# End of the second MLP: four plain blocks moved between the fifth and sixth block product, weights left unscaled, gate and residual one tile behind

## The chip, the core and the metric

The kernel runs on one core of a Trainium2 chip. The metric is device microseconds of one execution. A core has five engines, each with its own instruction queue, worked off in order: TensorE (PE in the profile, its weight loads PEld) multiplies matrices into PSUM, eight banks of 128 x 512 numbers; VectorE (DVE), ScalarE (ACT) and GpSimd (POOL) compute on tiles in SBUF, and only DVE and ACT read PSUM here; SyncE (SP) issues the loads. Stores of the output are issued on ACT's queue.

## What the kernel computes

A two-layer network over 1024 latent rows and 256 context rows of width 1024. Each layer has a token mixer and an MLP, each with a gated residual and a layer norm behind it. What this case is about is the very end, the MLP of the second layer, where only the latent rows are left:

```
h  = square(relu(modulate(x, sh2, sc2) @ w_up))      # 1024 x 4096
m  = h @ w_down                                      # 1024 x 1024
y  = alpha * x + g2 * m                              # g2: one row of 1024 gates, alpha = 2**0.5
out = (y - mean(y)) * rsqrt(var(y) + 1e-5) * ln2_g + ln2_b
```

## The kernel before

**Exact products from three.** Each float32 matrix is split into a rounded part "hi" and a rest "lo"; a product is three matmuls, hi x hi, hi x lo and lo x hi (`mm3`, lines 233 to 236). The split costs a copy on ACT and a subtraction (`lo`, line 230) on DVE or POOL.

**Block products.** `down_blocks` (it starts at line 2045) computes most of `h @ w_down` with seven products in place of eight per pair of blocks. The inner dimension is cut into seven groups (28 of the 32 slices of 128), and four slices are left for plain products at the end. In a group the seven products come in the order 1, 5, 6, 3, 2, 7, 4, each for four row tiles: 7 x 7 x 4 = 196 steps of six matmuls (128 x 512). `form` prepares the operands of a product two products ahead, with one or two POOL instructions, two ACT copies and a DVE subtraction. A step's result is added to the output half tile `acc` by DVE (`evac`, line 2237), two steps behind. Products 1, 6, 7 and 4 use the four banks x, products 5, 3 and 2 the four banks y; the banks keep running sums, so a step waits until the step before on its bank has been added to `acc`. Product 2 is the last that adds to row tiles 0 to 3; products 7 and 4 add to tiles 4 to 7.

**The order of the work.** Everything is under a manual schedule: each engine carries out its instructions in the order in which the program names them. Work of the end is hung onto the last steps by the dictionary `tail`, from step number (N is 196) to calls: loading and scaling the four last slices of `w_down`, splitting them and the four last slices of `h`, and the gate and residual of the first tiles.

**The end before.** `wm` (line 2179) multiplies a slice of `w_down` by the gate row on POOL (line 2182), then splits it. So the plain product comes out gated, and the gate must also be put on what the seven groups have summed: `fold` (line 2168) does it for one row tile, with a POOL multiplication (line 2171) and a DVE residual addition `alpha * x + y` (line 2172). `fold` of tiles 0 to 3 stands in `tail` at steps N-8, N-6, N-3 and N-2; that of tile t+4 at the head of tile t in `finish_last`. `finish_last` then does, for the eight row tiles in turn, 24 matmuls in two halves, DVE adds each half to `acc` (line 2335) and takes statistics (`bn_stats`, line 2336), `stats` (lines 1264 to 1270) makes mean and rstd with three small DVE and two small POOL instructions, ACT normalizes (line 2316), POOL multiplies by `ln2_g` (line 2318), DVE adds `ln2_b` (line 2321), and the tile is stored. The last tile ends on DVE alone (lines 2346 and 2348). The eight banks are used in turn.

**Buffers.** `s5` tiles (a in the profile) come from 25 buffers, `s4` tiles (b) from 20; a load waits until a buffer is free.

Of the kernel before, what the change touches and what calls it, by code (L numbers as in the profile page):

```python
# [10 lines left out]
F32 = mybir.dt.float32  # L11
F32R = mybir.dt.float32r
AF = mybir.ActivationFunctionType
ALU = mybir.AluOpType
# [4 lines left out]
D = 1024  # L19
SEQ = 1024  # L20
# [7 lines left out]
ALPHA = (2 * DEPTH) ** 0.25  # L28
# [49 lines left out]
def host_layout(a):  # L78
# [3 lines left out]
    o["xn"] = xa  # L82
    o["xT"] = xa.T.reshape(KT, 128, TOK)
    o["cT"] = np.stack([a["c"][0], a["c_ctx"]], 0).reshape(2, KT, 128).transpose(2, 1, 0)
# [18 lines left out]
    o["lnc"] = ln.reshape(2, 4, KT, 128).transpose(3, 0, 1, 2)  # L103
    o["sub"] = a["subln_w"].T
    o["dl"] = a["diff_lambda"].reshape(1, 512)
# [41 lines left out]
class Prog:  # L147
# [81 lines left out]
    def lo(self, out, x, hi, eng=None):  # L229
        (eng or self.nc.vector).tensor_tensor(out, x, hi, op=ALU.subtract)  # L230
# [181 lines left out]
    def first_xmod(self):  # L412
# [50 lines left out]
        def part(kt, u, k=0):  # L463
            for s, o in PS[u][k:]:
                self.mm3(o, W[u][0][:, kt], W[u][1][:, kt], X[kt][0][:, s], X[kt][1][:, s], kt == 0, kt == KT - 1)

# [10 lines left out]
        self.in_push(0)  # L477
        W = []
        for i in range(KT + 2):
# [3 lines left out]
            if i == 1:  # L483
                W = [self.wget(), self.wget()]
            loads(i + 2)
            if i == 2:
                W.append(self.wget())
            if i == 5:
# [34 lines left out]
    def pre(self, X, groups, per, ahead=0):  # L523
        ws = [self.wget() for _ in range(2)]
        self.wq_fill(ahead)
        ps = [None, None]
        for g in groups:
            if g is None:
                yield True
                continue  # L530
            for i, c, w in g:
                if ps[i] is None:
                    ps[i] = self.p3()
                for kt in range(KT):
                    xh, xl = X[kt]
                    self.mm3(ps[i][:, c:c + w], ws[i][0][:, kt], ws[i][1][:, kt], xh[:, c:c + w], xl[:, c:c + w],
                             kt == 0, kt == KT - 1)
                    if kt % per == per - 1:
                        yield False
        self.ready = ps  # L540
# [160 lines left out]
    def fourier2(self, b, n):  # L701
        nc = self.nc
        P = n // 256
        dm = self.dm
# [36 lines left out]
        for k in range(1, P):  # L741
# [3 lines left out]
            yield  # L745
        s2(P - 1)
        yield
# [370 lines left out]
    def attention_steps(self, l):  # L1118
# [34 lines left out]
        for i in range(N + LAG + 1):  # L1153
            T = []
            k = i - LAG
            if 0 <= k < N:
# [3 lines left out]
                E, Ec = st[k][0], st[k][2]  # L1160
                T = [self.att_T(E, Ec and Ec[0], st["aT", kh, kqb], kb, g) for g in range(3)]

            def t(g):
                if g < len(T):
                    next(T[g])

# [147 lines left out]
    def out_proj_setup(self, l):  # L1314
        nc = self.nc
        n = TOK if l == 0 else SEQ
        T = n // 128
        W, ld, gs, X2, xr, ys, s6, P = {}, {}, {}, [], {}, {}, {}, {}
        st = {}
# [24 lines left out]
        def mms(t, c, kts):  # L1344
# [7 lines left out]
            for kt in kts:  # L1352
                if kt not in W:
                    W[kt] = self.wget()
# [692 lines left out]
    def down_blocks(self, l, NG):  # L2047
        nc = self.nc
        n = SEQ if l else TOK
        T, HB, NB = n // 128, n // 2, D // 2  # L2050
        act, v, g = nc.scalar, nc.vector, nc.gpsimd
# [9 lines left out]
        acc = [None] * T  # L2061
# [82 lines left out]
        f = form(*seq[0])  # L2144
# [12 lines left out]
        bk = {"x": [self.p1() for _ in al], "y": [self.p1() for _ in range(8 - TH)]}  # L2157
        W, H, S, HR = [], [], [], []
        xr = {}
        self.acc = acc  # L2160
        gate = lambda t: self.gs[int(t >= 8)][:, :D]

        def rload(t):
            if t < T:
                xr[t] = self.s5()
                self.load(xr[t][:, :D], self.X2d[t])

        def fold(t):
            if t < T:
                y = acc[t]  # L2170
                g.tensor_tensor(y, y, gate(t), op=ALU.mult)
                v.scalar_tensor_tensor(y, xr.pop(t)[:, :D], ALPHA, y, op0=ALU.mult, op1=ALU.add)
                rload(t + 2)

        def wl(f):
            raw = self.s5()
            self.load(raw[:, :D], self.a["wd"][l, f])
            S.append(raw[:, :D])

        def wm():  # L2180
            raw = S.pop(0)
            g.tensor_tensor(raw, raw, gate(0), op=ALU.mult)
            hi, lo = self.s4(F32R), self.s4(F32R)
            act.copy(hi, raw)
            self.lo(lo, raw, hi)
            W.append((hi, lo))

        def whi():
            hi, lo = self.s4(F32R), self.s4(F32R)
# [7 lines left out]
        def hraw(f):  # L2197
            raw = self.s5()
            self.load(raw[:, :n], self.HL[f])
            HR.append(raw[:, :n])  # L2200

        def hconv():
            raw = HR.pop(0)
            hi, lo = self.s5(F32R), self.s5(F32R)
            act.copy(hi[:, :n], raw)
            self.lo(lo[:, :n], raw, hi[:, :n], g)
            H.append((hi, lo))

        def hl(f):
            hraw(f)  # L2210
            hconv()

        def gload(v=0):
            self.gs[v] = self.bcast(self.grow[(l, 5, v)], self.s5()[:, :D])

        n = SEQ if l else TOK
        N = len(prods)
        P = lambda fn, *a: (lambda: fn(*a))
        if l:
            tail = [[gload], [P(wl, 0)], [P(wl, 1), wm], [P(wl, 2), wm], [P(wl, 3), wm],  # L2220
                    [wm, P(rload, 0), P(rload, 1)], [P(hl, 0), P(hl, 1)], [P(fold, 0), P(hl, 2), P(fold, 1)],
                    [P(hl, 3), P(fold, 2), P(fold, 3)]]
            tail = {N - 4 * (9 - a) + b: f for a, fs in enumerate(tail) for b, f in enumerate(fs)}
        else:
            tail = {-20: P(wl, 0), -18: P(wl, 1), -16: whi, -15: wlo, -14: P(wl, 2), -13: whi, -12: wlo,
                    -11: P(hraw, 0), -10: whi, -9: wlo, -8: hconv, -7: P(hraw, 1), -6: P(wl, 3), -5: hconv,
                    -4: [P(hraw, 2), P(hraw, 3)], -3: [gload, P(rload, 0)], -2: hconv, -1: whi}
            tail = {N + k: f for k, f in tail.items()}
# [12 lines left out]
        for k, (n_, i, t) in enumerate(prods):  # L2241
# [8 lines left out]
            b, w = where(i, t)  # L2250
            ps = bk[b][w]
            evac(lag, ps)
            prod(n_, i, t, ps, i in (1, 5, 2))
            r, c = to[i]
# [9 lines left out]
                self.later()  # L2264
        evac(0)
        if l:
            self.lastW = W
            self.finish_last(l, H, lambda: None, bk["x"] + bk["y"], lambda t: fold(t + 4))
            yield
            return  # L2270
        wlo()
# [21 lines left out]
                self.wlo()  # L2293
            self.wrdy.append((hi, lo))

    def finish_last(self, l, H, lo, banks, pre):
        nc = self.nc
        T = SEQ // 128
        lg = self.bcast(self.a["lnr"][l, 2:3])
        lb = self.bcast(self.a["lnr"][l, 3:4])  # L2300
        W = self.lastW
        P = {}
        halves = (slice(0, 512), slice(512, 1024))

        def mm(t, c, r):
            sl = slice(128 * t, 128 * t + 128)
            if (t, c) not in P:
                P[t, c] = banks[(2 * t + c // 512) % 8]
            for i in r:
                self.mm3(P[t, c], H[i][0][:, sl], H[i][1][:, sl], W[i][0][:, c:c + 512], W[i][1][:, c:c + 512],  # L2310
                         i == 0, i == 3)

        def fin1(t):
            r, m, _ = st.pop(t)
            y = self.acc[t]
            nc.scalar.activation(y, y, AF.Identity, bias=m, scale=r)
            o[t] = self.s4()
            nc.gpsimd.tensor_tensor(o[t], y, lg, op=ALU.mult)

        def fin2(t):  # L2320
            nc.vector.tensor_tensor(o[t], o[t], lb, op=ALU.add)
            self.store(self.out[128 * t:128 * t + 128], o.pop(t))

        st, o = {}, {}
        for t in range(T):
            pre(t)
            y = self.acc[t]
            s6 = self.sm([128, 2, 6], bufs=3)
            if t == 0:
                mm(0, 0, range(3))  # L2330
                mm(0, 512, range(3))
                lo()
            for k, c in enumerate((0, 512)):
                mm(t, c, range(3, 4) if t == 0 else range(4))
                nc.vector.tensor_tensor(y[:, c:c + 512], P.pop((t, c)), y[:, c:c + 512], op=ALU.add)
                nc.vector.bn_stats(s6[:, k], y[:, c:c + 512])
                if k == 0 and t:
                    fin1(t - 1)
                if k == 0 and t > 1:
                    fin2(t - 2)  # L2340
            if t == T - 1:
                fin2(t - 1)
            st[t] = r, _, mean = self.stats(s6)
        x = self.s4()
        for c in halves:
            nc.vector.scalar_tensor_tensor(y[:, c], y[:, c], mean, lg[:, c], op0=ALU.subtract, op1=ALU.mult)
        for c in halves:
            nc.vector.scalar_tensor_tensor(x[:, c], y[:, c], r, lb[:, c], op0=ALU.mult, op1=ALU.add)
            self.store(self.out[128 * t:128 * t + 128, c], x[:, c])

    def finish(self, l):
        with self.tc.manual_schedule():
# [165 lines left out]
```

## Times and profile before

| what | us |
| --- | --- |
| median of three runs (lowest, highest) | 2947.97 (2942.29, 2949.51) |
| the profiled execution | 2943.8 |
| its span, first to last instruction | 2941.9 |
| PE busy in the span | 2743.8 (93%) |
| DVE busy | 2015.1 (68%) |
| ACT busy | 1149.9 (39%) |
| POOL busy | 1099.0 (37%) |

Times in the rows are microseconds from the start of the span. In a row of the timeline the columns are start, duration, engine, line, operation, output and inputs by kind of tile (q is a PSUM bank, a and b the SBUF tiles, c small ones), shape and count; in brackets the idle time before it and what ended it. A matmul row of 0.39 at the full clock overlaps the next, which starts 0.23 later. The last group's product 2 starts at 2849.28 and the plain blocks at 2875.54, where the output's input changes from a,a to b,a.

### The profile page before, as it was taken

What the parts mean: (1) busy time and instruction counts of PE and PEld (TensorE: products, weight loads), DVE (VectorE), ACT (ScalarE), POOL (GpSimd) and SP (SyncE); (2) the same over time, 40 slices, a digit from 0 to 9 for tenths busy, and PEclk for the clock granted to TensorE, in tenths of its full rate; (3) what the DMA queues carried; (4) which work ended last, traced back from release to release, by engine and by line L of the source; (5) the groups of instructions that cost most, each with busy time, mean ns of one, the idle gap of its engine ahead of it and who ended that gap; (6) DMA issues with size and microseconds to landing.
All of it is one profiled execution on the core that took longest, in us unless ns stands there. A gap on an engine that the chain in (4) does not pass through costs nothing.

```text
span 2941.9 us, 37767 instructions
## 1 busy us (share of the span) xinstructions
PE 2743.8 (93%) x14290; PEld 2347.7 (80%) x14290; DVE 2015.1 (68%) x2915; ACT 1149.9 (39%) x1608; POOL 1099.0 (37%) x664
## 2 busy tenths in 40 slices
PE   7889989889989999899999999999899999999986
PEld 5788878778779999788887788888777788878865
DVE  6667768845467787677776455667744677668887
ACT  4221156623343444533332321256523455553331
POOL 2511135633100000166665610146755000068795
PEclk9999999999999999999999999999899999999998
DMA  7244653337546555644344245662355565554451
GB/s 261 83 152 143 182 131 82 100 126 247 203 162 219 170 178 170 222 141 144 130 154 143 76 149 161 194 149 74 108 177 172 194 223 194 202 201 156 145 191 58
DMA packets 228745, 468.16 MB, mean 159 GB/s; under 512 B 18926, under 2 KB 116692, under 8 KB 228564
## 3 DMA queue, kind: packets, MB, share of 16 engines
q1 hardware_dynamic: 208392, 394.39, 41.5%
q10 hardware_dynamic: 17292, 61.93, 5.5%
q0 software_dynamic: 2880, 9.44, 0.8%
q8 instruction: 113, 1.85, 0.3%
q14 instruction: 68, 0.56, 0.1%
HBM read 322.36 MB, written 143.31 MB: 158 GB/s over the span
## 4 chain that ended last, share of the span: by engine, by line
PE 68%; DVE 11%; issue 6%; POOL 5%; DMA 5%; ACT 4%; SPq 1%; ACTq 0%; DVEq 0%; POOLq 0%
PE q L234 14%; PE q L236 14%; PE q L235 14%; PE p L234 5%; PE p L236 5%; PE p L235 5%; PE q L1025 3%; PE p L955 2%; PE p L956 2%; PE q L1012 2%; DVE c L958 2%; DVE a L230 1%; POOL a L230 1%; DVE b L230 1%; DMA d<-a 1%
## 5 line engine op out<-in xcount | busy, mean ns | idle before, releaser
L234 PE MATMUL q<-a,a 128*128 128x512 f32 (+1 forms) x1610 | 587.9, 365 | 34.9 <-DVE b L2237 13.7
L236 PE MATMUL q<-a,a 128*128 128x512 f32 (+2 forms) x1658 | 601.2, 363 | 5.0 <-DVE a L230 5.0
L235 PE MATMUL q<-a,a 128*128 128x512 f32 (+1 forms) x1594 | 581.6, 365 | 3.2 <-POOL a L230 3.2
L235 PE MATMUL p<-a,b 128*128 128x512 f32 (+1 forms) x1088 | 408.4, 375 | 1.1 <-POOL a L230 1.0
L234 PEld LDWEIGHTS q<-a,a 128*128 128x128 f32 x1610 | 305.2, 190 | 82.7 <-DVE t L1952 10.8
L236 PEld LDWEIGHTS q<-a,a 128*128 128x128 f32 x1658 | 314.2, 190 | 49.6 <-DVE a L230 7.4
L230 POOL TENSOR_TENSOR a<-b,a 128x256 fp32r<-128x256 f32 (+1 forms) x137 | 220.1, 1614 | 345.1 <-ACT a L2098 193.6
L2237 DVE TENSOR_TENSOR b<-q,b 128x512 f32<-128x512 f32 x405 | 268.7, 684 | 110.8 <-PE q L236 109.7
L235 PEld LDWEIGHTS q<-a,a 128*128 128x128 f32 x1594 | 302.4, 190 | 45.3 <-POOL a L230 4.3
L234 PE MATMUL p<-a,b 128*128 128x512 f32 (+1 forms) x816 | 307.7, 377 | 13.6 <-ACT b L2290 8.5
L236 PE MATMUL p<-a,b 128*128 128x512 f32 (+1 forms) x800 | 295.3, 369 | 4.0 <-DVE b L230 4.0
L230 DVE TENSOR_TENSOR a<-a,a 128x1024 fp32r<-128x1024 f32 (+4 forms) x163 | 266.7, 1639 | 38.3 <-ACT a L2095 27.5
L234 PE MATMUL q<-b,a 128*128 128x256 f32 (+1 forms) x748 | 256.7, 343 | 18.6 <-ACT b L604 8.4
L235 PE MATMUL q<-b,a 128*128 128x256 f32 (+1 forms) x748 | 253.8, 339 | 0.9 <-DVE b L230 0.9
L339 DVE SCALAR_TENSOR_TENSOR m<-w,k,m 128x256 f32<-128x256 f32 x448 | 227.4, 519 | 39.2 <-DMA w<-wmr 29.9
L236 PE MATMUL q<-b,a 128*128 128x256 f32 (+1 forms) x748 | 253.6, 339 | 0.0
L235 PEld LDWEIGHTS p<-a,b 128*128 128x128 f32 x1088 | 209.3, 192 | 34.2 <-POOL a L230 1.9
L958 DVE TENSOR_REDUCE c<-p 128x1 f32<-128x1280 f32 x128 | 190.5, 1488 | 63.1 <-PE p L956 61.9
L989 ACT ACTIVATE a<-p,c 128x1280 f32<-128x1280 f32 x128 | 170.4, 1331 | 89.8 <-DVE c L958 80.7
L234 PEld LDWEIGHTS p<-a,b 128*128 128x128 f32 x816 | 157.5, 193 | 39.3 <-ACT b L2290 9.3
L236 PEld LDWEIGHTS p<-a,b 128*128 128x128 f32 x800 | 153.9, 192 | 32.2 <-DVE b L230 7.0
L234 PEld LDWEIGHTS q<-b,a 128*128 128x128 f32 x748 | 144.8, 194 | 41.0 <-ACT b L604 11.4
(302 smaller groups left out, 5410.7 us busy)
## 6 DMA issues: line engine op xcount, KB each, us to landing
a<-d SPq DMA_DIRECT2D x86, 512.0 KB
w<-wmr SPq DMA_DIRECT2D x160, 256.0 KB
a<-d SPq DMA_DIRECT2D x56, 640.0 KB
b<-wu SPq DMA_DIRECT2D x64, 512.0 KB
d<-t SPq DMA_DIRECT2D x46, 640.0 KB
b<-wd SPq DMA_DIRECT2D x52, 512.0 KB
d<-a ACTq DMA_DIRECT2D x40, 640.0 KB
a<-d SPq DMA_DIRECT2D x80, 320.0 KB
```

The source lines that it names most:

```text
L230: (eng or self.nc.vector).tensor_tensor(out, x, hi, op=ALU.subtract)
L234: mm(out, lh, rh, start=start, stop=False, skip_group_check=on)
L235: mm(out, lh, rl, start=False, stop=False, skip_group_check=on)
L236: mm(out, ll, rh, start=False, stop=stop, skip_group_check=on)
L339: nc.vector.scalar_tensor_tensor(a, w[:, i], s, a, op0=ALU.mult, op1=ALU.add)
L955: nc.tensor.matmul(ps[:, c:c + w], Q[p][:, qs], K[p][0][:, ks], start=True, stop=False)
L956: nc.tensor.matmul(ps[:, c:c + w], Q[p][:, qs], K[p][1][:, ks], start=False, stop=True)
L958: nc.vector.reduce_max(mx, ps[:, :nkey], axis=AX.X, negate=True)
L989: self.nc.scalar.activation(e[:, :nkey], ps[:, :nkey], AF.Exp, bias=mx, accum_out=s)
L1012: nc.tensor.transpose(pt[:, i], e, self.ident)
L1025: nc.tensor.matmul(po[:, :256], V[i // 8][:, i % 8], aT[i // 4][:, i % 4], start=i == 0, stop=i == 9)
L2237: v.tensor_tensor(a, ps, a, op=ALU.add)
```

## The change

`wm` and `fold` go. The four slices of `w_down` are split unscaled (`whi`, `wlo`), and loads and splits of weights and `h` stand earlier in `tail`, from step N-26 to N-10. `finish_last` no longer does work when called: it returns `step`, and its calls are spread. After step N-9, the last of product 2, come the waiting additions and then the plain blocks of tiles 0 to 3 on the four banks y (steps 0 to 3 of `last`). Product 7 and 4 follow, with `last(4)` behind step N-8 and `last(5)` behind step N-6. After the loop come tiles 4 to 7 and the end, on all eight banks.

In a step for tile t, PE does the 24 matmuls and DVE adds the two halves; between the halves DVE does the residual of tile t-1; then come the statistics of tile t-1, the gate of tile t on POOL (now on the whole sum), the normalization and POOL's multiplication by `ln2_g` for tile t-1, and DVE's addition of `ln2_b` and the store for tile t-2. The last tile's gate and residual are on DVE, by halves. `ln2_g` and `ln2_b` lie in `s5` tiles, which are named before the loop over the steps.

```diff
-        gate = lambda t: self.gs[int(t >= 8)][:, :D]
...
-        def fold(t):
...
-        def wm():
...
         if l:
-            tail = [[gload], [P(wl, 0)], [P(wl, 1), wm], [P(wl, 2), wm], [P(wl, 3), wm],
-                    [wm, P(rload, 0), P(rload, 1)], [P(hl, 0), P(hl, 1)], [P(fold, 0), P(hl, 2), P(fold, 1)],
-                    [P(hl, 3), P(fold, 2), P(fold, 3)]]
-            tail = {N - 4 * (9 - a) + b: f for a, fs in enumerate(tail) for b, f in enumerate(fs)}
+            tail = {-26: P(wl, 0), -25: P(wl, 1), -24: whi, -23: [wlo, P(wl, 2)], -22: whi, -21: [wlo, P(wl, 3)],
+                    -20: whi, -19: [wlo, P(hraw, 0)], -17: P(hraw, 1), -16: hconv, -15: whi, -14: [wlo, hconv],
+                    -13: [gload, P(hraw, 2)], -12: P(hraw, 3), -11: hconv, -10: [hconv, P(rload, 0), P(rload, 1)]}
+            last = self.finish_last(l, H, W, xr, rload)
+            tail[-9] = [lambda: evac(0)] + [P(last, t, bk["y"]) for t in range(4)]
+            tail[-8], tail[-6] = P(last, 4), P(last, 5)
+            tail = {N + k: f for k, f in tail.items()}
...
         if l:
-            self.lastW = W
-            self.finish_last(l, H, lambda: None, bk["x"] + bk["y"], lambda t: fold(t + 4))
+            for k in range(7, 12):
+                last(k, bk["y"] + bk["x"])
...
+    def finish_last(self, l, H, W, xr, rload):
+        nc = self.nc
+        lg, lb = [self.sp.tile([128, 1280], F32, tag="s5", bufs=self.N5, name=self.nm("a"))[:, :D] for _ in range(2)]
...
+        def mm(t, banks):
+            sl = slice(128 * t, 128 * t + 128)
+            for k, c in enumerate(halves):
+                ps = banks[(2 * t + k) % len(banks)]
+                for i in range(4):
+                    self.mm3(ps, H[i][0][:, sl], H[i][1][:, sl], W[i][0][:, c], W[i][1][:, c], i == 0, i == 3)
+                y = self.acc[t][:, c]
+                nc.vector.tensor_tensor(y, ps, y, op=ALU.add)
+                if k == 0 and t % 4:
+                    resid(t - 1)
+        def resid(t):
+            y = self.acc[t]
+            nc.vector.scalar_tensor_tensor(y, xr.pop(t)[:, :D], ALPHA, y, op0=ALU.mult, op1=ALU.add)
+            rload(t + 2)
+        def stat(t):
+            s6 = self.sm([128, 2, 6], bufs=3)
+            for k, c in enumerate(halves):
+                nc.vector.bn_stats(s6[:, k], self.acc[t][:, c])
+            st[t] = self.stats(s6)
+        def gate(t):
+            y = self.acc[t]
+            nc.gpsimd.tensor_tensor(y, y, self.gs[0][:, :D], op=ALU.mult)
+        def norm(t):
+            r, m, _ = st.pop(t)
+            y = self.acc[t]
+            nc.scalar.activation(y, y, AF.Identity, bias=m, scale=r)
+            nc.gpsimd.tensor_tensor(y, y, lg, op=ALU.mult)
+        def shift(t):
+            y = self.acc[t]
+            nc.vector.tensor_tensor(y, y, lb, op=ALU.add)
+            self.store(self.out[128 * t:128 * t + 128], y)
+        def end(t):
+            y = self.acc[t]
+            x = xr.pop(t)
+            s6 = self.sm([128, 2, 6], bufs=3)
+            for k, c in enumerate(halves):
+                nc.vector.tensor_tensor(y[:, c], y[:, c], self.gs[0][:, c], op=ALU.mult)
+                nc.vector.scalar_tensor_tensor(y[:, c], x[:, c], ALPHA, y[:, c], op0=ALU.mult, op1=ALU.add)
+                nc.vector.bn_stats(s6[:, k], y[:, c])
+            r, _, mean = self.stats(s6)
+            for c in halves:
+                nc.vector.scalar_tensor_tensor(y[:, c], y[:, c], mean, lg[:, c], op0=ALU.subtract, op1=ALU.mult)
+            for c in halves:
+                nc.vector.scalar_tensor_tensor(y[:, c], y[:, c], r, lb[:, c], op0=ALU.mult, op1=ALU.add)
+                self.store(self.out[128 * t:128 * t + 128, c], y[:, c])
+        def step(n, banks=None):
+            h, k = divmod(n, 7)
+            t = 4 * h + k
+            if n == 0:
+                self.load(lg, self.a["lnr"][l, 2:3].to_broadcast([128, D]))
+                self.load(lb, self.a["lnr"][l, 3:4].to_broadcast([128, D]))
+            if k < 4:
+                mm(t, banks)
+            elif k == 4 and h == 0:
+                resid(t - 1)
+            if 0 < k < 5 and t < 8:
+                stat(t - 1)
+            elif h == 0 and k == 4:
+                stat(t - 1)
+            if k < 4 and t < 7:
+                gate(t)
+            if h and k == 4:
+                shift(t - 2)
+                end(t - 1)
+                return
+            if 0 < k < 5:
+                norm(t - 1)
+            if 1 < k < 6 and not (h and k > 4):
+                shift(t - 2)
+        return step
```

## Rows read from the trace of the kernel before

**Rows 1.** The page, part 2: span in 40 slices, PE busy and granted clock.
```profile
PE   7889989889989999899999999999899999999986
...
PEclk9999999999999999999999999999899999999998
```

**Rows 2.** Windows: stretch, length, busy PE, PEld, DVE, ACT, POOL, clock, DMA share, GB/s.
```profile
2849.20:2875.53 26.33, 22.02 (x72) 17.14 (x73) 22.05 (x18) 2.37 (x3) 24.56 (x10) 0.78 0.51 180
2875.53:2919.20 43.67, 43.67 (x193) 35.85 (x191) 31.09 (x43) 4.99 (x4) 20.70 (x16) 1.00 0.08 30
2919.20:2941.90 22.70, 0.04 (x1) 0.00 (x0) 16.55 (x32) 3.72 (x3) 12.11 (x12) 0.57 0.32 128
```

**Rows 3.** Timeline of PE: its three stops in the last group.
```profile
2841.59 0.39 PE L236 MATMUL q<-a,a 128*128 128x512 f32 x1
2849.28 0.76 PE L234 MATMUL q<-a,a 128*128 128x512 f32 x1 [7.30 <-DVE b L2237]
2849.84 0.63 PE L235 MATMUL q<-a,a 128*128 128x512 f32 x1
...
2863.56 0.47 PE L234 MATMUL q<-a,a 128*128 128x512 f32 x1 [0.90 <-DVE b L2237]
...
2868.49 0.80 PE L234 MATMUL q<-a,a 128*128 128x512 f32 x1 [3.33 <-DVE b L2237]
```

**Rows 4.** Timeline of DVE beside the second and third stop.
```profile
2858.81 3.40 DVE L2172 SCALAR_TENSOR_TENSOR b<-a,b 128x1024 f32<-128x1024 f32 x1 [2.23 <-POOL b L2171]
2862.14 1.27 DVE L2237 TENSOR_TENSOR b<-q,b 128x512 f32<-128x512 f32 x2
2864.48 3.36 DVE L2172 SCALAR_TENSOR_TENSOR b<-a,b 128x1024 f32<-128x1024 f32 x1 [1.07 <-POOL b L2171]
2867.76 1.88 DVE L2237 TENSOR_TENSOR b<-q,b 128x512 f32<-128x512 f32 x3
```

**Rows 5.** Chain of waits, one tile of the plain blocks: start, duration, work.
```profile
2884.60 2.35 POOL b L2171
...
2886.97 3.40 DVE b L2172
2890.37 0.61 DVE b L2335
...
2891.01 0.69 DVE c L2336
...
2893.05 0.22 DVE c L1264
...
2893.53 0.56 POOL c L1269
...
2894.35 2.35 POOL b L2171
```

**Rows 6.** Groups by line, POOL and ACT: count, busy, mean ns, idle before.
```profile
L2182 POOL TENSOR_TENSOR a<-a,a 128x1024 f32<-128x1024 f32 x4 | 11.5, 2880 | 0.0
...
L2316 ACT ACTIVATE b<-b,c,c 128x1024 f32<-128x1024 f32 x7 | 8.7, 1244 | 61.5 <-POOL c L1270 51.9 <-DMA out<-b 9.6
```

**Rows 7.** Timeline of POOL: last group's operands, and one tile's end.
```profile
2778.79 2.42 POOL L230 TENSOR_TENSOR a<-a,a 128x1024 fp32r<-128x1024 f32 x1 [1.16 <-ACT a L2098]
...
2813.43 2.39 POOL L2083 TENSOR_TENSOR a<-b,a 128x1024 f32<-128x1024 f32 x1
...
2886.91 2.39 POOL L2318 TENSOR_TENSOR b<-b,b 128x1024 f32<-128x1024 f32 x1
```

**Rows 8.** Timeline of the last 13 us, DVE and POOL.
```profile
2929.38 1.21 DVE L2321 TENSOR_TENSOR b<-b,b 128x1024 f32<-128x1024 f32 x1
2929.53 1.11 POOL L1270 TENSOR_TENSOR c<-c,c 128x1 f32<-128x1 f32 x1
...
2937.20 1.41 DVE L2348 SCALAR_TENSOR_TENSOR b<-b,c,b 128x512 f32<-128x512 f32 x2
```

**Rows 9.** Waits of the load queue, 2780 to 2870: total, times, longest.
```profile
SPq L222 <- PE q L236: 37.2, 8, 6.1
```

More of the change, by code (lines that the diff above doesn't have):

```diff
@@ L2166, in rload @@
                 self.load(xr[t][:, :D], self.X2d[t])
-        def fold(t):
[L2169 to L2173, printed above, removed]
         def wl(f):
@@ L2178, in wl @@
             S.append(raw[:, :D])
-        def wm():
[L2181 to L2186, printed above, removed]
         def whi():
@@ L2207, in hconv @@
             H.append((hi, lo))
-        def hl(f):
-            hraw(f)
-            hconv()
         def gload(v=0):
@@ L2294, in wconv @@
             self.wrdy.append((hi, lo))
-    def finish_last(self, l, H, lo, banks, pre):
+    def finish_last(self, l, H, W, xr, rload):
         nc = self.nc
[L2298 to L2302, printed above, removed]
+        lg, lb = [self.sp.tile([128, 1280], F32, tag="s5", bufs=self.N5, name=self.nm("a"))[:, :D] for _ in range(2)]
         halves = (slice(0, 512), slice(512, 1024))
-        def mm(t, c, r):
+        st, o = {}, {}
+        def mm(t, banks):
             sl = slice(128 * t, 128 * t + 128)
[L2307 to L2313, printed above, removed]
+            for k, c in enumerate(halves):
[19 more added lines that the diff above has]
+        def norm(t):
             r, m, _ = st.pop(t)
@@ L2316, in fin1 @@
             nc.scalar.activation(y, y, AF.Identity, bias=m, scale=r)
[L2317 to L2326, printed above, removed]
-            y = self.acc[t]
-            s6 = self.sm([128, 2, 6], bufs=3)
[L2329 to L2349, printed above, removed]
+            nc.gpsimd.tensor_tensor(y, y, lg, op=ALU.mult)
+        def shift(t):
+            y = self.acc[t]
+            nc.vector.tensor_tensor(y, y, lb, op=ALU.add)
+            self.store(self.out[128 * t:128 * t + 128], y)
```

## Prediction

> **What bounds the kernel now.** I read the slices of the page first. PE is at 9 tenths in nearly every slice but the last, where busy share and clock fall [rows 1]. So until the end only PE's work counts, and the change adds and takes away no matmul. Then the windows of the end [rows 2]: 72 matmuls of the last twelve block steps take 26.33 us, 22.02 busy at a mean clock of 0.78; the 192 of the plain blocks take 43.67, which is 0.2265 each, PE's pace without stops; then 22.70 us pass without PE. So two things can be won or lost: PE's stops before the last matmul, and the path from there to the end.
>
> The timeline of PE shows the stops: 7.30, 0.90 and 3.33 us, each ended by line 2237, the addition that frees the bank [rows 3]. DVE's timeline beside them shows why the addition was late: it stood in DVE's queue behind a residual addition that itself waited for a gate on POOL and then took 3.40 us [rows 4]. After the stops of 7.30 and 3.33 matmuls start 0.43 apart for about 12 matmuls, in place of 0.2265, so each costs a further 2.4 us; after 0.90 they do not. The last group's first 24 product-2 matmuls thus end at 2849.28 + 12 x 0.43 + 12 x 0.2265, about 2857.1.
>
> The chain of waits shows the second limit [rows 5]. One plain tile goes: gate on POOL 2.35, residual on DVE 3.40, addition 0.61, statistics, two small POOL instructions, next gate; from gate to gate 9.75 us, where PE needs 24 x 0.2265 = 5.44. The residual takes 3.40 because POOL's `ln2_g` multiplication started at 2886.91 [rows 7], 0.06 before it, and it ends 1.07 after POOL does; without POOL beside it such a DVE instruction takes 1.21, or 1.13 from end to end in a queue [rows 8]. The two take SBUF in turn. PE runs ahead of this chain on eight banks, so before the change it costs PE nothing in the plain blocks.
>
> **The change part by part.** I count from E, the moment when product 2 ends and plain block 0 can start.
>
> *Up to E.* Four POOL multiplications of weights go, 11.5 us busy [rows 6], and the splits stand some steps earlier. PE without a stop would be at E = 2841.82 + 5.44 = 2847.3. But block 0 now needs all splits at E, not 10.9 us of products later. From 2815.8, when the last group's first operand is formed [rows 7], POOL has 11 multiplications or subtractions before it (five rests of products 6, 3, 2, 7 and 4, two operands, four rests of `h`), 11 x 2.36 = 26.0, and DVE nine subtractions with both inputs in SBUF (five rests, four weights), 9 x 1.13 = 10.2. In turn that is 36.2, to 2852.0; three or four waits of 1.16 for ACT's copy [rows 7] make it 2856. The ends are 2847.3 and 2860; I take 2856, against 2857.1 before. So this part gains 1 us; most of the stop of 7.30 moves a few steps on.
>
> *Plain blocks 0 to 3.* Block 0's matmuls end at E + 5.44; 0.17 until DVE starts, addition 0.61, gate 2.35: gate 0 is done at E + 8.6. Block 1 ends at E + 10.9; addition, statistics of tile 0 (two of 0.71 and three small, 0.50), POOL's small ones 0.82, gate 2.35: gate 1 at E + 16.75. From there the chain of [rows 5] sets the pace, in the new order: residual 3.42 with its start, addition 0.61, statistics 1.42 + 0.50, small POOL 0.82, gate 2.35, and DVE's `ln2_b` addition, which starts together with the small ones and holds them up by 0.92, as the 1.11 in place of 0.19 shows [rows 8]. That is 10.04 a tile, so gate 3 ends at E + 36.8. PE needs 21.75 for the four blocks and finds its four banks free, since their additions come early in each step.
>
> *Products 7 and 4.* PE does product 7's four steps by E + 27.2. Product 4's first step needs the addition of product 7, tile 0. In DVE's queue that stands behind `last(4)`: residual 3 (3.42 after gate 3), statistics 1.92, `ln2_b` of tile 2 1.13, then 0.61: E + 43.9. PE stops for 16.7 us. This is the wait of [rows 4], with a longer chain ahead of it. The next bank's addition stands behind `last(5)`: small POOL instructions with their hold-up until E + 43.9, normalization on ACT 1.24 [rows 6], `ln2_g` 2.39, `ln2_b` 1.13, addition 0.61: E + 49.3. Then three steps, 4.1, and 2.4 of half clock: product 4 ends at S = E + 55.8. Unstopped it would be E + 32.6.
>
> *Tiles 4 to 7.* The same pace once more: gate 4 at S + 8.6, gate 5 at S + 16.75, gate 6 at S + 26.8. Then residual 6 3.42, addition of the last half 0.61, statistics 1.92, small POOL 0.82 + 0.92, normalization 1.27, `ln2_g` 2.39, `ln2_b` 1.15: S + 39.3. Last tile: two halves of gate, residual and statistics, 0.67 + 0.67 + 0.71 each, 4.1; small 0.45; four half instructions, 2.7 (1.41 for two [rows 8]): S + 46.5. From the end of DVE at 2938.6 [rows 8] to the span's end the store takes 3.3, so S + 49.8.
>
> Nothing else is on the path. The loads of residual tiles and of `ln2_g`, `ln2_b` are issued on SP tens of microseconds before use; if a buffer is late, a load waits for a product to end, 6.1 at most [rows 9], and that is the second rival. Stores stand on ACT's queue behind `ln2_b`, which DVE does before the next statistics, so ACT waits in time that it has.
>
> *Sum.* The span ends at E + 55.8 + 49.8 = 2856 + 105.6 = 2961.6, against 2941.9: 19.7 us more. Before, from its E of 2857.1 it took 84.8. The profiled execution took 2943.8, 4.2 under the median of 2947.97; I add the 20 to the median: 2968. The ends are E at 2847.3 (11.0 more) and at 2860 (23.7 more).
>
> **The rivals.**
>
> *PE is not stopped, and it is faster.* If the tiles kept PE's pace of 5.44, product 7's additions would come in time, S = E + 32.6, and the span would end at E + 82.4: 2938.4 with E of 2856, 3.5 less, which is no change; with E of 2847.3 2929.7, 12.2 less, which is faster. For it: the weight scaling is gone, and only three gates are left behind the last product. Against it: gate, residual and statistics were at 9.75 a tile, and the change keeps this order. It decides from the point where the first addition of product 7 is done by E + 27.2, 16.7 earlier than worked out. No change 0.04, faster 0.06.
>
> *Loads come later: slower still.* The two new `s5` tiles are named before the loop. If they hold buffers from there, 23 of 25 are left, and each operand's load or copy can wait for the next product to end. Waits of this kind are up to 6.1 [rows 9]; one product takes 5.44. That sets E 5.4 later, 25 us more than before. Against it: the buffers are first written at step 0. 0.15.
>
> *The residual gets SBUF first.* Gate's end lets both the residual and `ln2_g` go. If DVE came first, the residual would take 1.13, and `ln2_g` would fit behind the statistics: 7.75 a tile. That saves 2.3 at gates 2, 3 and residual 3, and at gate 6 and residual 6, 11.5 in all: 8.2 us more than before, on the edge of what shows. Against it: with both ready at the same gate, POOL was first [rows 5, 7]. The Trainium skill (SBUF — State Buffer, section Who interferes with whom) says that DVE with two SBUF inputs and GpSimd lock each other out and that "issue order, not op shape, decides who blocks". By that rule a slightly earlier DVE would bring this case; the trace agrees with the lock, 3.40 against 1.21. 0.10, half of it slower.
>
> **How the numbers follow.** The forecast, 16 to 24 more, has 0.65; the rivals 0.10, 0.15 and 0.10. About 0.3%, 8.8 us, is what can be told from no change here. Slower: 0.65 + 0.15 + 0.05 = 0.85; same: 0.04 + 0.05 = 0.09; faster 0.06. The range runs from 7 to 30 more, 2955 to 2978: it takes in the second and third rival and both ends of E, and leaves out the first.
>
> **What would show it.** In the profile after: line 2182 and its 11.5 us gone; POOL subtractions close together up to the plain blocks; a PE stop of some 17 us, ended by the addition of product 7's first step, before product 4, a second of about 3, half clock behind both; 10 us from gate to gate in tiles 1 to 3 and 5 to 6; about 28 us from the last matmul to the span's end, in place of 22.7. The prediction is wrong if PE goes through product 4 without a long stop, if the residuals take 1.2, or if POOL does not set the pace.

## The result and the profile after

The changed kernel takes 2966.83 us (median of 4 runs, 2963.23 to 2969.07), the kernel before beside it 2948.74 (2942.29 to 2950.94): a ratio of 1.0064 with a 95% interval of 1.0048 to 1.0080, 18.1 us slower. The forecast was 2968, 20 more. The profiled execution took 2965.72, its span is 2963.8.

The two executions can't be laid on each other from the span's start. The operand subtraction of line 2079 stands in both kernels ahead of all the work that the change moves, but for the load of the gate row, and its last one comes 4.06 us later after the change (the first one on POOL, in the first layer, is 3.41 later already, 1250.88 for 1247.47):

```profile
2806.18 3.39 POOL L2079 TENSOR_TENSOR a<-b,b 128x1024 f32<-128x1024 f32 x1
```

is the kernel before, and

```profile
2810.24 3.38 POOL L2079 TENSOR_TENSOR a<-b,b 128x1024 f32<-128x1024 f32 x1
```

the one after (timeline of POOL: start, duration). From this start to the span's end it is 135.7 us before and 153.6 after, 17.9 more. All places below are told from it and called "after the last operand"; it agrees with the medians and leaves the shift of the unchanged code out.

The page's slices, beside [rows 1]: the last of the 40 has PE at 4 tenths and a clock of 6, before it was 6 and 8.

```profile
PE   7899999889989999899998999999899999999994
...
PEclk9999999999999999999999999999999999999996
```

PE's stops, beside [rows 3]. Two small ones stand before the first two steps of product 2, and a long and a short one before the first two steps of product 4:

```profile
2849.95 0.47 PE L234 MATMUL q<-a,a 128*128 128x512 f32 x1 [3.15 <-DVE b L2220]
...
2853.18 0.80 PE L234 MATMUL q<-a,a 128*128 128x512 f32 x1 [0.90 <-DVE b L2220]
...
2859.37 0.39 PE L234 MATMUL q<-b,a 128*128 128x512 f32 x1
...
2902.69 0.79 PE L234 MATMUL q<-a,a 128*128 128x512 f32 x1 [15.93 <-DVE b L2220]
2903.28 0.63 PE L235 MATMUL q<-a,a 128*128 128x512 f32 x1
2903.71 0.63 PE L236 MATMUL q<-a,a 128*128 128x512 f32 x1
...
2908.33 0.79 PE L234 MATMUL q<-a,a 128*128 128x512 f32 x1 [2.72 <-DVE b L2220]
```

The row with q<-b,a is the first plain matmul; it is E, 49.1 after the last operand. Behind the stop of 15.93 the matmuls start 0.43 apart, as before behind the stop of 7.30.

What PE waited for is in DVE's queue. Line 2220 is the addition that frees a bank, 2300 the residual, 2306 the statistics, 2321 the addition of `ln2_b`:

```profile
2895.74 3.35 DVE L2300 SCALAR_TENSOR_TENSOR b<-a,b 128x1024 f32<-128x1024 f32 x1 [3.00 <-POOL b L2311]
2899.12 1.29 DVE L2306 BATCH_NORM_STATS2 c<-b 128x6 f32<-128x512 f32 x2
...
2900.82 1.22 DVE L2321 TENSOR_TENSOR b<-b,a 128x1024 f32<-128x1024 f32 x1
2901.95 0.68 DVE L2220 TENSOR_TENSOR b<-q,b 128x512 f32<-128x512 f32 x1
2906.46 1.22 DVE L2321 TENSOR_TENSOR b<-b,a 128x1024 f32<-128x1024 f32 x1 [3.82 <-POOL b L2317]
2907.60 2.47 DVE L2220 TENSOR_TENSOR b<-q,b 128x512 f32<-128x512 f32 x4
```

The first matmul of each stop starts 0.7 us behind the start of its addition (2901.95 to 2902.69, 2907.60 to 2908.33). Ahead of that the chain of waits runs through one row tile after another, beside [rows 5] (start, duration, work; line 2311 is the gate, 2294 the plain addition, 1269 the first small instruction on POOL):

```profile
2883.58 2.36 POOL b L2311
2885.96 3.36 DVE b L2300
2889.32 0.60 DVE b L2294
2889.93 1.20 DVE c L2306 x2
...
2891.63 1.53 POOL c L1269
...
2893.41 2.30 POOL b L2311
```

From gate to gate 9.83 us, while PE needs 5.44 a tile. The seven gates start 7.86, 9.87, 9.83, 27.36, 7.83 and 9.88 apart. The long gap stands before gate 4, where it is the chain that waits for PE, which has first to do product 4 and plain block 4 behind its stop:

```profile
2920.72 2.40 POOL L2311 TENSOR_TENSOR b<-b,a 128x1024 f32<-128x1024 f32 x1 [14.29 <-DVE b L2294]
```

The windows beside [rows 2] (stretch, length, busy PE, PEld, DVE, ACT, POOL, granted clock, DMA share, GB/s): the end of product 7 with product 4, the other four plain blocks, the end.

```profile
2885.00:2914.30 29.30, 10.65 (x32) 7.71 (x31) 18.49 (x23) 2.48 (x2) 13.62 (x9) 0.65 0.16 65
2914.30:2936.10 21.80, 21.80 (x97) 17.83 (x95) 12.01 (x16) 1.25 (x1) 7.85 (x5) 1.00 0.00 1
2936.10:2963.80 27.70, 0.13 (x1) 0.00 (x0) 17.18 (x28) 2.48 (x2) 11.62 (x9) 0.56 0.19 76
```

Products 7 and 4 are 48 matmuls, 10.9 us at PE's pace, and end 29.3 us behind 2885.00; and 27.7 us pass behind the last matmul's end, 22.7 before.

### The profile page after: what moved, and what is told of

It reads as the page before. It is cut to its first block, busy times and chain, and to the rows that moved or that the text cites. A ratio compares the mean times of both kernels' runs of the same rounds, so it can differ in the third digit from the quotient of the medians.

```text
span 2963.8 us, 37774 instructions
## 1 busy us (share of the span) xinstructions
PE 2750.2 (93%) x14290; PEld 2352.7 (79%) x14290; DVE 2013.0 (68%) x2918; ACT 1149.9 (39%) x1608; POOL 1084.9 (37%) x659
## 5 line engine op out<-in xcount | busy, mean ns | idle before, releaser
L234 PEld LDWEIGHTS q<-b,a 128*128 128x128 f32 x748 | 144.4, 193 | 42.1 <-ACT b L604 11.1
```

The source lines that it names most:

```text
L234: mm(out, lh, rh, start=start, stop=False, skip_group_check=on)
```

## The experiments

Two theories. **The chain:** gate, residual and statistics of seven row tiles, one after another at some 9.85 us, set the pace from the first plain block to the end; PE's stop is only the place where this shows, and what is saved there comes back behind the last matmul unless the chain gets shorter. **The stop:** the loss is PE's 18.65 us of stops and the half clock behind them; without them the time is that of before or less. A third, from the prediction's rivals: loads come late because the rows `ln2_g` and `ln2_b` hold buffers.

Each ratio is to the kernel before as it ran beside that kernel: its median was 2948.74 beside the changed kernel, 2946.37 beside the next four and 2946.99, the one in the table, beside the last four. The two last columns are from the profiled executions; the last counts from the last matmul's start.

| kernel | median, us | ratio (95%) | last operand to end | last matmul to end |
| --- | --- | --- | --- | --- |
| before | 2946.99 | 1 | 135.7 | 23.0 |
| changed | 2966.83 | 1.0064 (1.0048, 1.0080) | 153.6 | 28.0 |
| two steps behind | 2959.27 | 1.0037 (1.0025, 1.0049) | 144.3 | 32.4 |
| all blocks at the end | 2959.42 | 1.0044 (1.0028, 1.0060) | 149.6 | 48.2 |
| gate ahead | 2957.86 | 1.0032 (1.0017, 1.0046) | 144.4 | 23.8 |
| rows named late | 2963.47 | 1.0061 (1.0040, 1.0081) | 154.3 | 28.0 |
| gate ahead, spread | 2948.96 | 1.0008 (0.9999, 1.0018) | 135.3 | 32.1 |
| no gate | 2948.23 | 1.0001 (0.9992, 1.0010) | 134.7 | 20.8 |
| before, no scaling | 2939.03 | 0.9972 (0.9961, 0.9982) | 128.2 | 23.0 |
| best | 2938.04 | 0.9970 (0.9960, 0.9980) | 128.9 | 23.3 |

**Two steps behind.** The two steps without matmuls, which stand in the queues between product 7's first steps, go behind product 4.

```diff
-            tail[-8], tail[-6] = P(last, 4), P(last, 5)
...
-            for k in range(7, 12):
+            for k in (4, 5, 7, 8, 9, 10, 11):
```

> The changed kernel with one thing moved: step 4 and step 5 of the end (residual, statistics and ln2_b of tiles 2 and 3) stand behind the last block step instead of behind the first and third step of product 7, so that product 7's additions stand ahead of them in DVE's queue. Theory A (the chain of gate, residual and statistics sets the pace, 9.85 us a tile, and PE's stop is only where it shows): the first stop in product 4 falls from 15.9 to 7 to 8 us, since steps 0 to 3 still stand ahead, the second of 2.7 goes; the chain of tile 3 goes on beside product 4; 10 to 12 us less than the changed kernel, about 2956. Theory B (PE's stop is the loss, whatever the chain does): the same stops, and all of 8 + 2.7 + 2.4 of half clock comes back: 13 less, 2954. Told apart by the next run, not by this one.

Measured: 9.3 us less than the changed kernel from the last operand on, 7.6 by the medians, a little under what either theory gave. Only one stop is left in products 7 and 4:

```profile
2889.27 0.79 PE L234 MATMUL q<-a,a 128*128 128x512 f32 x1 [6.64 <-DVE b L2219]
```

PE's stops fell from 18.65 to 6.64, by 12.0, and one stretch of half clock went, so the last matmul starts 13.7 earlier (111.9 after the last operand for 125.6); but 4.4 of it came back behind it, 32.4 for 28.0. What the two steps do is still to be done, later.

**All blocks at the end.** The four plain blocks and the two steps go behind product 4.

```diff
-            tail[-9] = [lambda: evac(0)] + [P(last, t, bk["y"]) for t in range(4)]
-            tail[-8], tail[-6] = P(last, 4), P(last, 5)
...
-            for k in range(7, 12):
+            for k in (0, 1, 2, 3, 4, 5, 7, 8, 9, 10, 11):
```

> The changed kernel with the four plain blocks put back behind product 4: steps 0 to 5 and 7 to 11 in a row on all eight banks. Weights stay unscaled, gate and residual a tile behind. Theory A: PE has no stop from product 2 to the last matmul, which comes some 25 us earlier than in the changed kernel, but the tiles still take 9.8 us each from gate to gate, seven of them, so that the stretch from the last matmul to the end grows from 27.7 to 48 to 52, and the time falls by only 2 to 5 us: about 2963. Theory B: the whole stop comes back, 15.9 + 2.7 + 4.8 of half clock, less what the tail already had: 19 to 23 less, about 2946.

This is the run that tells the two apart. PE now has no stop behind the second step of product 2; this is its last:

```profile
2850.82 0.60 PE L234 MATMUL q<-a,a 128*128 128x512 f32 x1 [0.34 <-DVE b L2218]
```

The last matmul starts 101.4 after the last operand, 24.2 earlier than in the changed kernel. And yet the end comes only 4.0 earlier, because 48.2 us pass behind it. (By the medians it is 7.4 earlier, and the intervals of the two ratios overlap, so the 4.0 rests on the traces; a gain of 19 to 23 is excluded by both.) The stop as the whole cause is refuted: the chain is as slow when PE does not wait. Gates 1 to 3 stand 9.87 and 9.88 apart here, 9.87 and 9.83 in the changed kernel:

```profile
2880.26 2.40 POOL L2309 TENSOR_TENSOR b<-b,a 128x1024 f32<-128x1024 f32 x1
...
2890.13 2.40 POOL L2309 TENSOR_TENSOR b<-b,a 128x1024 f32<-128x1024 f32 x1
...
2900.01 2.39 POOL L2309 TENSOR_TENSOR b<-b,a 128x1024 f32<-128x1024 f32 x1
```

The run moves one thing more. The first plain matmul, and with it the chain, comes 9.0 later (58.1 after the last operand for 49.1), and the gap before gate 4 shrinks from 27.36 to 15.67. So the stop is not free: it opens a gap in the chain. What it is worth with the chain starting early, the spread run below shows.

**Gate ahead.** In each step the gate of the new tile is put on POOL before the statistics of the tile before, and that tile's residual behind both additions. So the chain no longer goes through the gate of one tile to the statistics of the last and back.

```diff
-                if k == 0 and t % 4:
-                    resid(t - 1)
...
-            if 0 < k < 5 and t < 8:
-                stat(t - 1)
...
             if k < 4 and t < 7:
                 gate(t)
+            if 0 < k < 5 and t < 8:
+                resid(t - 1)
+                stat(t - 1)
```

> The changed kernel with another order inside a step, blocks where the change has them: the gate of tile t stands on POOL ahead of the small instructions of tile t-1, and the residual of tile t-1 stands on DVE behind both additions of tile t. The same instructions, so a gate no longer waits for the statistics of the tile before. Theory A: 7.6 to 8 us from gate to gate instead of 9.85 (two POOL multiplications, the small ones and two DVE instructions in turn), first stop 11 to 13, second about 1; 12 to 16 us less, about 2953. Theory B, in the form that the place in DVE's queue is what counts: the same instructions stand ahead of product 7's additions, so 0 to 3 less, about 2965.

Measured: 9.2 less than the changed kernel, and 8.7 and 8.0 us from gate 1 to gate 2 and from there to gate 3. The chain's theory had the direction and missed the size. Two views show why, DVE's and POOL's timeline in one tile:

```profile
2876.89 3.39 DVE L2319 TENSOR_TENSOR b<-b,a 128x1024 f32<-128x1024 f32 x1 [0.48 <-POOL b L2315]
2880.21 1.27 DVE L2294 TENSOR_TENSOR b<-q,b 128x512 f32<-128x512 f32 x2
2881.41 1.21 DVE L2298 SCALAR_TENSOR_TENSOR b<-a,b 128x1024 f32<-128x1024 f32 x1
```

```profile
2873.56 3.30 POOL L2315 TENSOR_TENSOR b<-b,a 128x1024 f32<-128x1024 f32 x1 [1.36 <-ACT b L2314]
2876.82 2.38 POOL L2309 TENSOR_TENSOR b<-b,a 128x1024 f32<-128x1024 f32 x1
2879.16 1.52 POOL L1269 TENSOR_TENSOR c<-c,k 128x1 f32<-128x1 f32 x1
```

The residual (line 2298) now takes 1.21. But the end of POOL's `ln2_g` multiplication (line 2315) lets two instructions go: the gate behind it on POOL, and DVE's `ln2_b` addition (line 2319), which starts 0.07 later and takes 3.39. The wait for SBUF has moved from one DVE instruction to another in the same queue. PE still stops for 11.39 and 2.10.

**Rows named late.** The two buffers for `ln2_g` and `ln2_b` are named in step 0, not before the loop.

```diff
-        lg, lb = [self.sp.tile([128, 1280], F32, tag="s5", bufs=self.N5, name=self.nm("a"))[:, :D] for _ in range(2)]
+        lg = lb = None
...
             if n == 0:
+                lg, lb = [self.s5()[:, :D] for _ in range(2)]
```

> The changed kernel with the two tiles of ln2_g and ln2_b named at step 0 instead of before the loop over the steps, nothing else. If the two hold buffers from before the loop (rival of the prediction), loads and copies of the last groups come earlier now and plain block 0 starts 3 to 5 us earlier: about 2962. If a buffer is held only from the first write, nothing changes: within 1 us in the trace, plain block 0 as far behind the start of the last group as in the changed kernel.

Measured: the first plain matmul 48.3 after the last operand (49.1 in the changed kernel), the same stops of 15.93 and 2.72, 154.3 to the end. So the buffers cost nothing that can be seen, and the rival of the later loads falls. The load queue's longest wait for PE (total, times, longest) is the same 9.8 in the changed kernel and in the one before, where it stands in another row than that of [rows 9]; with the rows named late it is 24.1, 4, 9.8 as in the changed kernel. The row before and the one after:

```profile
SPq L222 <- PE q L235: 19.0, 3, 9.8
```

```profile
SPq L222 <- PE q L235: 24.1, 4, 9.8
```

**Gate ahead, spread.** On top of the gate ahead, the plain blocks are put among the steps of products 7 and 4.

```diff
-            tail[-9] = [lambda: evac(0)] + [P(last, t, bk["y"]) for t in range(4)]
-            tail[-8], tail[-6] = P(last, 4), P(last, 5)
+            tail[-9] = [lambda: evac(0), P(last, 0, bk["y"])]
+            tail[-7], tail[-5], tail[-3] = [P(last, t, bk["y"]) for t in (1, 2, 3)]
+            tail[-1] = [P(last, 4), P(last, 5)]
```

> Order of the third experiment (each gate on POOL ahead of the statistics of the tile before, the residual behind both halves), and the plain blocks spread as well: block 0 behind step N-9, blocks 1, 2 and 3 behind N-7, N-5 and N-3, the two steps without matmuls behind N-1. If the chain of gate, residual and statistics is what costs, and PE's stop only the place where it shows, then the products 7 and 4 that now lie between the plain blocks give each tile 10.9 us of matmuls, more than the 8.0 to 8.7 a tile that the chain took in the third experiment: no stop over 3 us in the product steps, the last product's steps end some 14 us earlier than there, and 15 to 20 us are gained on the changed kernel, which is about the time of the kernel before. If it is the stop alone that costs, the third experiment's 11.39 and 2.10 go here, and with 24 us or so behind the last matmul the gain on the changed kernel is 20 to 24 us, a few us below the kernel before. If the time stays within 3 us of the third experiment, neither holds.

Measured: 18.3 less than the changed kernel from the last operand on, 17.9 by the medians, the time of before. The expectation's 10.9 us of matmuls a tile was wrong: a plain block and two steps are 36 matmuls, 8.15 us. The first three gates indeed stand 8.16 apart, PE's pace, and only the fourth comes 8.77 behind:

```profile
2861.60 2.40 POOL L2310 TENSOR_TENSOR b<-b,a 128x1024 f32<-128x1024 f32 x1 [4.10 <-DVE b L2295]
2869.76 3.31 POOL L2310 TENSOR_TENSOR b<-b,a 128x1024 f32<-128x1024 f32 x1 [5.76 <-DVE b L2295]
...
2877.92 3.31 POOL L2310 TENSOR_TENSOR b<-b,a 128x1024 f32<-128x1024 f32 x1 [0.31 <-DVE b L2295]
...
2886.69 3.38 POOL L2310 TENSOR_TENSOR b<-b,a 128x1024 f32<-128x1024 f32 x1
```

PE has no stop over 0.3 us from the first plain matmul on: the stops of together 13.49 and their half clock are gone, and the last matmul starts 17.4 earlier than with the gate ahead alone (103.2 after the last operand for 120.6). Of these 17.4, 8.3 went into the end, 32.1 for 23.8, and 9.1 are left: without the stop, and with the chain's early start kept, about half of what PE wins comes through. With PE at its pace throughout, the chain still sets the end, and the time is no better than before.

**No gate.** The changed kernel without POOL's multiplication of tiles 0 to 6.

```diff
-            if k < 4 and t < 7:
-                gate(t)
```

> The changed kernel with the gate's multiplication of row tiles 0 to 6 left out (what it puts out is not the reference's). It takes the seven POOL multiplications of 2.35 to 2.40 us out of the chain. If that chain sets the pace, a tile takes about 7.5 us in place of 9.85: the stop of 15.93 before product 4 shrinks to 4 to 8 us, the three tiles behind it gain 2.4 each, and the whole is 14 to 25 us below the changed kernel, so near the kernel before or a few us under it. If the gate is hidden beside other work, the gates' places are filled by what DVE and ACT do and the time falls by less than 5 us.

Measured: 18.9 less from the last operand on, 18.6 by the medians. The stops before product 4 are 4.02 and 2.39, the residual takes 1.22, and POOL's `ln2_g` multiplications (line 2317) of three tiles now stand 5.06 and 5.00 apart, less than PE's 5.44 and than the 7.5 a tile expected:

```profile
2884.90 2.40 POOL L2317 TENSOR_TENSOR b<-b,a 128x1024 f32<-128x1024 f32 x1 [1.36 <-ACT b L2316]
...
2889.96 2.34 POOL L2317 TENSOR_TENSOR b<-b,a 128x1024 f32<-128x1024 f32 x1 [1.36 <-ACT b L2316]
...
2894.96 2.35 POOL L2317 TENSOR_TENSOR b<-b,a 128x1024 f32<-128x1024 f32 x1 [1.35 <-ACT b L2316]
```

So the seven gates, 16.7 us of POOL, cost the changed kernel 18.9, somewhat more than their own time; the residuals behind them also took 3.39 in place of 1.22.

**Before, no scaling.** The kernel before without line 2182.

```diff
-            g.tensor_tensor(raw, raw, gate(0), op=ALU.mult)
```

> The kernel before with the four multiplications of the weight slices by the gate row left out (what it puts out is not the reference's; the gate and residual of the row tiles stay as they were). It measures by itself what the change removes at this place: 11.5 us of POOL. If POOL's queue is what makes PE stop for 7.30 us before product 2, that stop shrinks to 2 to 4 us, the other two stay within 2 us of what they were, and the time falls by 3 to 7 us. If the stop comes from the gate and residual of tiles 0 and 1 that stand in the queue there, it stays over 6 us and the time within 2 us. My prediction gave this part 1 us in the changed kernel, where the splits stand earlier at the same time.

Measured: 7.5 less from the last operand on, ratio 0.9972; a little more than expected. The stop of 7.30 is 1.00, and the half clock behind it is gone:

```profile
2843.66 0.47 PE L234 MATMUL q<-a,a 128*128 128x512 f32 x1 [1.00 <-DVE b L2236]
```

Product 2 ends 42.4 after the last operand, 50.9 before: 8.5 won there, and 2.3 lost again in the next stop, 3.18 for 0.90, a little more than the 2 that were expected; the first plain matmul comes 7.6 earlier, 61.8 for 69.4.

**Best.** What the chain's theory points to: order and spread as above, weights and `h` loaded and split from step N-32 on, and POOL relieved.

```diff
-            nc.gpsimd.tensor_tensor(y, y, self.gs[0][:, :D], op=ALU.mult)
+            (nc.vector if t in (0, 4) else nc.gpsimd).tensor_tensor(y, y, self.gs[0][:, :D], op=ALU.mult)
...
+            if t in ND:
+                r, _, mean = st[t]
+                nc.vector.scalar_tensor_tensor(y, y, mean, lg, op0=ALU.subtract, op1=ALU.mult)
+                return
```

with `ND = (3, 4, 6)`, and for these tiles a second such instruction with rstd and `ln2_b`.

> The version that the theory of the chain points to: order and spread as in the spread run, loads and splits of weights and h from step N-32 on, gates of row tiles 0 and 4 on DVE in place of POOL, and normalization, ln2_g and ln2_b of tiles 3, 4 and 6 by two DVE instructions in place of one each on ACT, POOL and DVE. It takes up to 2.4 us of POOL out of the chain at five places. If the chain on POOL and DVE sets the pace, it is 20 to 30 us below the changed kernel and 3 to 10 below the kernel before. If what is left is PE's own pace and the stops before product 2, it lies with the spread run, within 3 us.

Measured: ratio 0.9970, 9 us below the kernel before and 29 below the changed one by the medians, both in the expected bounds. Against the spread run it is 6.4 less from the last operand on. The first plain matmul comes 4.7 earlier (43.7 for 48.5), but PE does not keep that: in plain block 0 it waits twice, 0.64 and 3.65, for POOL's last splits of `h`, with half clock behind the second stop, and the last matmul starts 2.4 later than in the spread run (105.6 for 103.2).

```profile
2866.89 0.79 PE L236 MATMUL q<-b,a 128*128 128x512 f32 x1 [3.65 <-POOL a L230]
```

The whole gain lies behind the last matmul, 23.3 for 32.1. The earlier splits and the relief of POOL were not tried one by one; in this trace the earlier splits show no gain beyond plain block 0.

## Why the prediction was right, step by step

**Up to E.** Predicted 2856. Measured 2859.37, less the 4.06 by which the unchanged code was late: 2855.3. That the splits on DVE and POOL hold PE up was right: the addition that ends the stop of 3.15 stands behind a subtraction that takes 3.38 beside POOL's, where one alone takes 1.22.

```profile
2845.84 3.38 DVE L230 TENSOR_TENSOR a<-a,a 128x1024 fp32r<-128x1024 f32 x1
2849.13 0.68 DVE L2220 TENSOR_TENSOR b<-q,b 128x512 f32<-128x512 f32 x1
```

But the sum takes E as the end of all splits, and that did not set it. (The operand at 2815.8 from which it counts is product 6's, line 2083; the group's first one is line 2079's.) The wait stayed at the first two steps of product 2 (3.15 and 0.90, with 3.1 of half clock behind them) and did not move on; the last split ends 2.2 us behind E:

```profile
2859.23 2.39 POOL L230 TENSOR_TENSOR a<-a,a 128x1024 fp32r<-128x1024 f32 x1
```

So the agreement within 0.7 is in part luck. In five other runs with the same code up to here the first plain matmul comes earlier, 47.5 to 48.5 after the last operand, and PE then waits 0.3 to 1.2 in plain block 0 for that split. With the gate ahead:

```profile
2858.61 0.50 PE L236 MATMUL q<-b,a 128*128 128x512 f32 x1 [1.16 <-POOL a L230]
```

What such a small gain hides was not worked out: taking away the scaling alone is worth 8.5 at this place, and the change won 1.7 of it. The likely reason, which no run tried by itself, is that the splits of `h` now have to be done by plain block 0, before products 7 and 4. The best version, whose weight loads and splits stand three to seven steps earlier and which differs from the spread run in nothing else up to here, has its first plain matmul at 43.7 where the spread run is at 48.5, and then waits for the splits of `h`.

**The pace of the tiles.** Predicted: gate 0 done at E + 8.6, gate 1 at E + 16.75, 10.04 a tile, gate 3 at E + 36.8. Measured, from the starts of line 2311 and their durations: E + 8.8, E + 16.7, 9.87 and 9.83, E + 36.3. The term that was new, the hold-up of POOL's small instruction by `ln2_b` on DVE, was taken at 0.92 and is 0.96 (1.52 for 0.56):

```profile
2872.87 0.56 POOL L1269 TENSOR_TENSOR c<-c,k 128x1 f32<-128x1 f32 x1 [4.67 <-DVE c L1268]
...
2873.66 2.40 POOL L2311 TENSOR_TENSOR b<-b,a 128x1024 f32<-128x1024 f32 x1
2876.01 2.39 POOL L2317 TENSOR_TENSOR b<-b,a 128x1024 f32<-128x1024 f32 x1
2881.79 1.52 POOL L1269 TENSOR_TENSOR c<-c,k 128x1 f32<-128x1 f32 x1 [3.39 <-DVE c L1268]
```

**The stops.** First step of product 4 at E + 43.9, stop 16.7; second at E + 49.3. Measured E + 43.3 and 15.93; E + 49.0 and 2.72. Product 4 ends at E + 54.9, 55.8 predicted. The half clock behind both stops was there, a granted clock of 0.65 in the window from 2885.00.

**The end.** From there 49.8 predicted, 49.5 measured; 28 from the last matmul, 27.7 to 28.0 measured.

**The sum.** 19.7 more predicted, 17.9 measured in the traces: 0.7 too much at E, 0.9 in the chain, 0.3 in the end.

**The rivals.** "PE is not stopped" fell at its point of decision: product 4's first step, which waits for the first addition of product 7, started at E + 43.3, and the point was E + 27.2. "Loads come later" fell with the rows named late; its "up to 6.1" was the longest of one row of the load queue's waits, and another has 9.8. "The residual gets SBUF first" did not happen in the changed kernel, and what decides it can be seen: POOL's `ln2_g` multiplication starts at 2876.01, the residual at 2876.09, and it takes 3.39. With the gate ahead, the order is turned in tiles 1 and 5; in tile 1 the residual of tile 0 starts 0.16 before POOL's gate, and it is the gate that takes longer:

```profile
2867.94 1.22 DVE L2298 SCALAR_TENSOR_TENSOR b<-a,b 128x1024 f32<-128x1024 f32 x1
```

```profile
2868.10 3.32 POOL L2309 TENSOR_TENSOR b<-b,a 128x1024 f32<-128x1024 f32 x1 [3.04 <-DVE b L2294]
```

This is what the Trainium skill says (SBUF — State Buffer, section Who interferes with whom), that the order of issue decides who blocks; the traces agree, 3.39 for DVE in the one order and 3.32 for POOL in the other, with 0.08 and 0.16 us between the starts.

**What the prediction did not say.** It worked out the chain, but gave PE's stop as the largest term and did not ask what would be left of the loss without the stop. The stop is mostly where the loss shows. The run with all blocks at the end takes it away, and of the 24.2 that PE wins 4.0 are left; the run without gates leaves PE's work as it is and gains 18.9. The two also wait for each other in turn: PE 15.93 and 2.72 for the chain before product 4, then the chain 14.29 for PE before gate 4; the spread run, which lays the products between the tiles, has no such stop and is 9.1 less than the gate ahead alone. Before, four of the eight gates stood beside the products of the last group, where PE had other work, and four in the plain blocks; the change puts seven, with their residuals, behind the first plain block, at 9.85 a tile against PE's 5.44, and for the first four has only the 10.9 us of products 7 and 4 to lay beside the difference.

## What to carry to other kernels

Before matmul work is moved to give an elementwise chain more cover, work out the chain's own time per tile, with its waits for SBUF, and compare it with PE's: if it is the longer one, moving the matmuls only moves the place where PE waits. Take work out of the chain, or out of the queue that holds up the additions that free the banks, and spread the tiles so that PE's work per tile is at least the chain's. And measure what is removed by itself: here the removed scaling was worth some 8 us, which the rest of the same change hid.

## What the runs showed of the hardware that was not expected

The same unchanged code took different times in different executions. The first subtraction of line 2079 on POOL, ahead of everything that any of these kernels changes, starts between 1246.5 (rows named late) and 1255.9 us (best). Single spans, 2944.7 for the best version and 2941.9 for the one before, would have turned the order of the two round; the medians and the distance from the last operand agree on 7 to 9 us the other way.

A stop of 1.00 left the matmuls behind it 0.23 apart; behind 3.15, in the changed kernel, they fell to 0.43 from the fourth matmul on and were still there behind the next stop, of 0.90. From 2849.95 to E product 2 takes 9.42, of which 5.44 is PE's pace and 0.90 the stop: 3.1 of half clock, where it was 2.3 behind the stop of 7.30 (7.77 less 5.44). In five other runs with the same code up to there, where the second stop was 0.3 to 0.5, the half clock took 1.8 to 3.0. So what it costs behind the same stop differs from one execution to the next.
